# Self attention that begins seven steps earlier among the projections, with another order of passes in its weighted values

## The chip, the cores and the metric

The kernel runs on one core of one Trainium2 chip. The metric is the device time of one execution in microseconds (us). The core's engines are named as the profile names them: PE (TensorE, the matrix engine; PEld is its weight load), DVE (VectorE), ACT (ScalarE), POOL (GpSimd) and SP (SyncE, which here issues most DMAs).

## The reference

One decoder block on x (512 tokens of width 1024), all in float32. The part that the change touches first is a causal differential attention with four heads; each head has two score maps of 64 dimensions and 128 value dimensions:

```python
h = rms_norm(x, g_mix)
u, q, k, v, gate_logits = split(h @ w_in)
y_pool = causal_multiscale_pool(u, w_pool, pool_scale)
q, k = apply_rope(q), apply_rope(k)
p = softmax(where(mask, q·k / 8, -1e30))      # two maps per head
a = p[0] - lam * p[1]
o = rms_norm(a @ v, g_subln) * (1 - lam_init)
x = x + (concat(y_pool, o) * sigmoid(gate_logits)) @ w_out
```

A cross attention to a memory of 256 tokens follows (four heads of 256 dimensions), then a squared-ReLU MLP of width 4096, each behind an RMS norm and added to x, and a last RMS norm.

## The kernel before

**Data.** Activations lie transposed: 128 features on the partitions, the 512 tokens along the free axis. Every float32 operand is split into a high part, rounded to the matrix engine's fp32r type, and a low part, the rest; a product is three passes, high x high, high x low and low x high (`mm3`, L104). `split` (L110) makes the two parts, a copy on ACT (L111) and a subtraction on DVE (L112). The same is done for every block of weights (`prep`), after a DMA on SP's queue (`fetch`, L149), two tiles ahead of its use.

**Steps and tiles.** PE's order is written out by hand; the order of the other engines is planned by the framework from an estimate of when each instruction could run, earlier lines first, and `tc.high_priority()` ranks the instructions traced under it ahead of others. The planned orders are fixed when the kernel is built. A projection tile is eight steps of `mm3` (`tile_mm`, L290) into one of two PSUM banks `acc`. Each step advances a counter (`tick`), and work that `after(steps, ...)` has put on a list is issued on PE between two steps when its count is reached.

**The stage around the change.** `v_proj` (L375) makes the values in four PSUM banks (three `sc`, one `av`); three steps later `stats` (L394) computes the norm's factors, multiplies them into the cosine and sine tables and scales the values into `vr` (L264, L265). Then the tiles of `PLAN` (L41) run in order: k and q per head, the gates g, the pooling inputs u. `qk_proj` (L412) rotates a tile: four copies on ACT that swap quarters (L417), one product on DVE (L418), a product and a sum on POOL (L419, L420), two casts on ACT (L423, L425) and two subtractions on DVE (L424, L426). For k a swapped copy `z` is made by two DMAs on SP's queue (L430, L431). These halves share a ring of six buffers (`s`).

Behind the first two tiles, `START` steps on, the 16 blocks of scores (four heads, four blocks of 128 queries) are put on the list, `SPACE` = 6 steps apart. `scores` (L435) takes two PSUM banks of the three called `sc`; DVE adds the mask and finds the minimum (L445), ACT takes the exponential (L447), DVE inverts the sum (L449, L450), ACT scales one map (L451) and DVE combines the two (L452). `SOFTMAX` = 15 steps later `flip` (L456) transposes the block on PE (L463) and splits it into `at[0]` and `at[1]`; `ATTEND` = 3 steps after a head's last flip `attend` (L469) multiplies it with the values into the bank `av`, and `FINISH` = 6 steps later `finish` (L481) normalises and `merge` (L509) applies the gate. A gate tile costs ACT four passes (L500 to L504) and DVE two (L498, L503); a u tile works on DVE and POOL (L532 to L543).

**Cross attention.** For each head `cross_scores` (L673) makes scores and softmax, `cross_transpose` (L696) transposes and splits the result into a buffer `at`, and `cross_out` (L709) multiplies it with the memory's values into two `acc` banks, which are split into `xg`. The last of these calls are written out at L738 to L745.

Of the kernel before, what the change touches and what calls it, by code (L numbers as in the profile page):

```python
# [17 lines left out]
P = 128  # L18
# [3 lines left out]
NT = T // P  # L22
# [6 lines left out]
LAM_INIT = 0.8 - 0.6 * math.exp(-0.3 * 0)  # L29
WINDOWS = (2, 4, 8, 16)  # L30
PAD = 16
START, SPACE, SOFTMAX, ATTEND, FINISH, POOLING = 20, 6, 15, 3, 6, 23
MEMIN, EARLY, LATE = 16, [4, 5, 6, 0, 1], [2, 7, 3]
WARM = 8
ON_POOL = (1, 3, 5, 7), (1, 3, 5)
# [2 lines left out]
PARTS = "A11", "A12", "A21", "A22"  # L38
ORDER = "A11", "A12", "s1", "s2", "s3", "A22", "s4"
FIRST_ORDER = "A11", "s1", "A12", "s2", "s3", "A22", "s4"  # L40
PLAN = "k0 q0 q1 k1 q2 q3 g4 k2 g5 g6 k3 g7 u0 u1 u2 u3 g0 g1 g2 g3"  # L41

G_MIX, G_CROSS, G_MEM, G_MLP, G_FINAL, PSCALE, GSUB, LAMS = 0, 8, 16, 24, 32, 40, 44, 45
NG_COL = LAMS
# [6 lines left out]
def block_kernel(ctx: ExitStack, tc: tile.TileContext, x0g, xT, memT, wv, wm, wst, wckv, wpool, vecs, csts, outT):  # L51
    nc = tc.nc
# [23 lines left out]
    def sb(tag, shape, bufs, dt=F32):  # L76
        p = apool if tag in EARLY_TAGS else late["pool"] if tag in LATE_TAGS else pool
        return p.tile(shape, dt, tag=tag, name=nm(tag), bufs=bufs)

    def tmp(dt=F32):  # L80
        return sb("tmp", [P, T], 10, dt)

    def small(n=1):
        return sb("small", [P, 4], 24)[:, :n]

    def pair(tag, bufs):
        return sb(tag, [P, 2, T], bufs, F32R)

    def ps(tag, bufs):
        return psum.tile([P, T], F32, tag=tag, name=nm(tag), bufs=bufs)  # L90

    def acc():
        return ps("acc", 2)

    def f(ap):
        return ap.bitcast(F32)
# [7 lines left out]
    def mm3(o, lh, ll, rh, rl, start, stop):  # L104
        nc.tensor.matmul(o, lh, rh, start=start, stop=False)  # L105
        nc.tensor.matmul(o, lh, rl, start=False, stop=False)  # L106
        nc.tensor.matmul(o, ll, rh, start=False, stop=stop)  # L107
# [97 lines left out]
    def weights(i):  # L205
        far = 4 if i >= FIRST_UP else 0
        for j in range(i, i + 4 + far):
            if j < FIRST_UP or late:
                load(j)
        for j in range(i, i + 3 + far // 2):  # L210
            if j < FIRST_UP or late:
                prep(j)
        return ready.pop(i)


    def rsqrt(dst, ssum, scale, v, l, by=None):

        V.tensor_scalar(v, ssum, scale, EPS, op0=ALU.mult, op1=ALU.add)
        S.activation(l, ssum, AF.Ln, bias=eps, scale=scale)
        S.activation(dst, l, AF.Exp, scale=-0.5)  # L220
        S.activation(l, dst, AF.Square)
        V.scalar_tensor_tensor(l, l, -0.5, v, op0=ALU.mult, op1=ALU.mult)
        if by is not None:
            by(dst)
        V.scalar_tensor_tensor(dst, l, 1.5, dst, op0=ALU.add, op1=ALU.mult)

    def split_sq(sq, w, eng=V):
        hi = tmp(F32R)[:, :w]
        lo = tmp(F32R)[:, :w]
        split(hi, lo, sq, eng)  # L230
        return hi, lo

    def bcast_sum(o, hi, lo):
        nc.tensor.matmul(o, ones, hi, start=True, stop=False)
        nc.tensor.matmul(o, ones, lo, start=False, stop=True)
# [35 lines left out]
    def after(steps, fn, *args):  # L271
        heapq.heappush(due, (clock[0] + steps, uid[0], fn, args))
        uid[0] += 1
# [6 lines left out]
    def tick(n=1):  # L280
        for _ in range(n):
            clock[0] += 1
            run_due()
# [6 lines left out]
    def tile_mm(o, w, rhs, ks=range(KC), first=True, last=True):  # L290
        ks = list(ks)
        for n, k in enumerate(ks):
            c = slice(k * P, (k + 1) * P)
            mm3(o, w[0][:, c], w[1][:, c], rhs[k][0], rhs[k][1],
                first and n == 0, last and n == len(ks) - 1)
            tick()
# [5 lines left out]
    plan = [(e[0], int(e[1])) for e in  # L302
            PLAN.split()]
    where = {}
# [23 lines left out]
    def W(*key):  # L328
        return weights(where[key])
# [5 lines left out]
    st = {}  # L335
# [76 lines left out]
    def qk_proj(which, h):  # L412
        o = acc()
        tile_mm(o, W(which, h), xg)
        a, b = tmp(), tmp()
        for j in range(4):
            S.copy(b[32 * (j ^ 1):32 * (j ^ 1) + 32, :], o[32 * j:32 * j + 32, :])  # L417
        V.tensor_tensor(a, o, cos_r, op=ALU.mult)  # L418
        ROPE_E.tensor_tensor(b, b, sin_r, op=ALU.mult)  # L419
        nc.gpsimd.tensor_tensor(a, a, b, op=ALU.add)  # L420
        s = pair("s", 6)
        top, bot = slice(0, 64), slice(64, 128)
        S.copy(s[top, 0, :], a[top, :])  # L423
        V.tensor_tensor(s[bot, 0, :], a[top, :], f(s[top, 0, :]), op=ALU.subtract)  # L424
        S.copy(s[bot, 1, :], a[bot, :])  # L425
        V.tensor_tensor(s[top, 1, :], a[bot, :], f(s[bot, 1, :]), op=ALU.subtract)  # L426
        st[which, h] = s
        if which == "k":
            z = pair("s", 6)
            nc.sync.dma_start(f(z[top, :, :]), f(s[bot, :, :]))  # L430
            nc.sync.dma_start(f(z[bot, :, :]), f(s[top, :, :]))  # L431
            st["z", h] = z
# [36 lines left out]
    def attend(h):  # L469
        at = st["at", h]  # L470
        o = ps("av", 1)
        e = slice(h * P, (h + 1) * P)
        for b in range(NT):
            vh, vl = st["v"][b]
            mm3(o[:, b * P:], vh[:, e], vl[:, e], at[0][:, b, b * P:], at[1][:, b, b * P:],
                b == 0, b == NT - 1)
        sq = tmp()
        S.activation(sq, o, AF.Square)
        sp = split_sq(sq, T)

        def finish():  # L481
            s = ps("tr", 2)
            bcast_sum(s, *sp)
            y = tmp()
            rsqrt(y, s, 1.0 / P, sq, tmp(),
                  lambda r: V.scalar_tensor_tensor(r, o, st["gsub"], r, op0=ALU.mult, op1=ALU.mult))
            merge(4 + h, y)

        after(FINISH, finish)
# [19 lines left out]
    def merge(m, y):  # L509
        eng = MERGE_E if m < 4 else V  # L510
        eng.tensor_tensor(y, y, gate.pop(m), op=ALU.mult)
        pr = pair("mix", 8)
        split(pr[:, 0, :], pr[:, 1, :], y, MLO_E if m < 4 else V)
        mixed[m] = (pr[:, 0, :], pr[:, 1, :])
# [158 lines left out]
    def cross_scores(h):  # L673
        es = []
        for j in range(NT // 2):
            o = ps("sc", 3)
            for b in range(2):
                i = 2 * j + b
                tb = slice(i * P, (i + 1) * P)
                for c in range(2):  # L680
                    q, k = st["cq", 2 * h + c], st["mk", 2 * h + c]
                    mm3(o[:, b * M:(b + 1) * M], q[0][:, tb], q[1][:, tb], k[0], k[1], c == 0, c == 1)
            mx, sm = small(2), small(2)
            V.tensor_reduce(mx, o.rearrange("p (b m) -> p b m", b=2), axis=AX.X, op=ALU.max, negate=True)
            e = tmp()
            for b in range(2):
                c = slice(b * M, (b + 1) * M)
                S.activation(e[:, c], o[:, c], AF.Exp, bias=mx[:, b:b + 1], accum_out=sm[:, b:b + 1])
            V.reciprocal(sm, sm)
            for b in range(2):  # L690
                c = slice(b * M, (b + 1) * M)
                V.tensor_scalar(e[:, c], e[:, c], sm[:, b:b + 1], None, op0=ALU.mult)
            es.append(e)
        st["p", h] = es

    def cross_transpose(h):  # L696
        t = sb("at", [P, NT, T], 2, F32R)
        pt = (t[:, :MT, :], t[:, MT:, :])
        for j, e in enumerate(st["p", h]):
            tr = ps("tr", 2)  # L700
            for c in range(MT):
                for b in range(2):
                    nc.tensor.transpose(tr[:, (2 * c + b) * P:(2 * c + b + 1) * P],
                                        e[:, b * M + c * P:b * M + (c + 1) * P], ident)
            src = tr.rearrange("p (c t) -> p c t", c=MT)
            split(pt[0][:, :, j * M:(j + 1) * M], pt[1][:, :, j * M:(j + 1) * M], src)
        st["pt", h] = pt

    def cross_out(h):  # L709
        pt = st["pt", h]  # L710
        for dc in range(2):
            o = acc()
            m = 2 * h + dc
            c = slice((m % 4) * P, (m % 4) * P + P)
            for i in range(MT):
                vh, vl = st["mv", m // 4, i]
                mm3(o, vh[:, c], vl[:, c], pt[0][:, i, :], pt[1][:, i, :], i == 0, i == MT - 1)
            pr = pair("xg", 8)
            split(pr[:, 0, :], pr[:, 1, :], o)
            cross_o[m] = (pr[:, 0, :], pr[:, 1, :])  # L720
# [5 lines left out]
    for m in range(KC):  # L726
        o = acc() if m else ps("sc", 3)
# [9 lines left out]
            after(2, cross_transpose, m // 2 - 1)  # L737
    flush()  # L738
    cross_out(0)
    cross_scores(3)  # L740
    cross_transpose(2)
    cross_out(1)
    cross_out(2)
    after(2, cross_transpose, 3)
# [181 lines left out]
    for g in range(NG):  # L926
# [3 lines left out]
        for m in range(KC):  # L930
# [13 lines left out]
            if m < 2:  # L944
                o = acc()
# [8 lines left out]
            o = acc()  # L954
# [75 lines left out]
```

## Time and profile before

| | us |
|---|---|
| median of three runs | 722.4 (722.18 to 723.12) |
| the profiled execution | 722.57 |
| its span, first to last instruction | 720.8 |

The mean granted clock of PE is 0.998 of full speed. In a row of the timeline the first number is the start from the beginning of the span, the second the duration, both in us; a bracket at the end gives the idle time before the instruction and who ended it. A product's duration is modelled and longer than the distance to the next one, since PE overlaps them: with 512 columns it shows 0.39 us, and the next begins 0.23 us after it. In the view of waits a row reads: engine, tile and line that waited, for whom, us in total, times, the longest. In a view by stage a row gives busy time and instructions (x) of PE, PEld, DVE, ACT and POOL, then clock, share of the DMA engines and GB/s.

### The profile page before, as it was taken

Reading aid. Unit: us, or ns where it says so; the run is one execution under the profiler, and the core shown is the slowest. Engines: PE = TensorE matmul, PEld = TensorE weight load, DVE = VectorE, ACT = ScalarE, POOL = GpSimd, SP = SyncE. Lnnn points to the kernel's source line nnn. Section 1 sums busy time; section 2 is a strip of 40 time slices with the busy share of each in tenths; the row PEclk is TensorE's granted clock in tenths of the full one; section 3 lists DMA queues with packets and bytes.
Section 4 is the critical chain, followed back from the end, with each engine's and each line's share of the span. In section 5 each row is a group of like instructions: output and inputs, shape, how many; then the busy total and the mean of one; then the engine's idle time right before and its main releaser. Section 6 shows DMA issues by size and latency. Waiting matters only on the chain.

```text
span 720.8 us, 10378 instructions
## 1 busy us (share of the span) xinstructions
PE 706.5 (98%) x4016; PEld 617.0 (86%) x4016; DVE 510.6 (71%) x797; ACT 392.5 (54%) x646; POOL 66.9 (9%) x59
## 2 busy tenths in 40 slices
PE   8999999999999999999999999999999999999995
PEld 6887888788889888888879988999889988899894
DVE  7698999975888546572999954598446973589525
ACT  7498998676766434452865641355214641256432
POOL 0044112534000000000000000000000000000000
PEclk9999999999999999999999999999999999999999
DMA  8443223143525552113924850558216661305103
GB/s 315 151 118 116 88 75 116 60 146 119 176 88 176 181 170 83 65 58 143 246 79 127 237 164 30 150 111 294 89 33 167 205 182 58 88 30 161 45 1 116
DMA packets 28257, 91.09 MB, mean 126 GB/s; under 512 B 3089, under 2 KB 5137, under 8 KB 28209
## 3 DMA queue, kind: packets, MB, share of 16 engines
q1 hardware_dynamic: 25856, 81.92, 33.5%
q0 software_dynamic: 2352, 8.52, 7.0%
q8 instruction: 31, 0.51, 0.3%
q14 instruction: 18, 0.14, 0.1%
HBM read 86.24 MB, written 2.10 MB: 123 GB/s over the span
## 4 chain that ended last, share of the span: by engine, by line
PE 89%; DVE 5%; ACT 4%; issue 1%; DMA 0%; POOL 0%; DVEq 0%; SPq 0%; ACTq 0%
PE acc L105 17%; PE acc L106 17%; PE acc L107 17%; PE sc L105 11%; PE sc L106 11%; PE sc L107 11%; ACT tmp L447 1%; PE sc L386 1%; PE sc L388 1%; PE sc L390 1%; DVE tmp L445 1%; DVE wlo L112 1%; ACT tmp L417 1%; ACT whi L111 1%; DMA wraw<-wv 0%
## 5 line engine op out<-in xcount | busy, mean ns | idle before, releaser
L111 ACT CAST whi<-wraw 128x1024 fp32r<-128x1024 f32 (+1 forms) x94 | 97.2, 1035 | 107.5 <-PE acc L106 41.0
L105 PE MATMUL acc<-xg,whi 128*128 128x512 f32 x392 | 155.0, 395 | 0.0
L107 PE MATMUL acc<-xg,wlo 128*128 128x512 f32 x392 | 153.0, 390 | 0.0
L106 PE MATMUL acc<-xg,whi 128*128 128x512 f32 x392 | 152.7, 390 | 0.0
L112 DVE TENSOR_TENSOR wlo<-wraw,whi 128x1024 fp32r<-128x1024 f32 (+1 forms) x94 | 115.1, 1226 | 26.8 <-ACT whi L111 26.4
L107 PEld LDWEIGHTS acc<-xg,wlo 128*128 128x128 f32 x392 | 73.6, 188 | 15.8
L105 PEld LDWEIGHTS acc<-xg,whi 128*128 128x128 f32 x392 | 73.7, 188 | 14.5
L106 PEld LDWEIGHTS acc<-xg,whi 128*128 128x128 f32 x392 | 73.7, 188 | 14.3
L572 DVE TENSOR_TENSOR vr<-acc,vr 128x512 f32<-128x512 f32 x39 | 26.9, 690 | 76.5 <-PE acc L107 76.4
L105 PE MATMUL sc<-mix,whi 128*128 128x256 f32 (+1 forms) x184 | 54.2, 295 | 0.0
L107 PE MATMUL sc<-mix,wlo 128*128 128x256 f32 (+1 forms) x184 | 54.1, 294 | 0.0
L106 PE MATMUL sc<-mix,whi 128*128 128x256 f32 (+1 forms) x184 | 54.0, 294 | 0.0
L164 POOL DMA_DIRECT2D mraw<-wst x16 | 13.8, 864 | 429.1 <-DMA mraw<-wst 302.3
L111 ACT CAST whi<-mraw 128x1024 fp32r<-128x1024 f32 x24 | 25.0, 1052 | 45.9 <-PE acc L106 33.0
L890 DVE TENSOR_TENSOR tmp<-sc,tmp 128x512 f32<-128x512 f32 x56 | 37.5, 684 | 6.5 <-PE sc L107 6.4
L111 ACT CAST mhl<-wraw 128x1024 fp32r<-128x1024 f32 x19 | 20.0, 1052 | 34.4 <-PE acc L106 18.0
L106 PE MATMUL acc<-xg,mhl 128*128 128x512 f32 x96 | 37.4, 390 | 0.0
L105 PE MATMUL acc<-xg,mhl 128*128 128x512 f32 x96 | 37.4, 389 | 0.0
L107 PE MATMUL acc<-xg,mhl 128*128 128x512 f32 x96 | 37.4, 389 | 0.0
L107 PEld LDWEIGHTS sc<-mix,wlo 128*128 128x128 f32 x184 | 34.5, 188 | 1.1
L105 PEld LDWEIGHTS sc<-mix,whi 128*128 128x128 f32 x184 | 34.6, 188 | 1.0
L106 PEld LDWEIGHTS sc<-mix,whi 128*128 128x128 f32 x184 | 34.5, 187 | 1.1
(274 smaller groups left out, 1731.4 us busy)
## 6 DMA issues: line engine op xcount, KB each, us to landing
wraw<-wm SPq DMA_DIRECT2D x76, 512.0 KB, 3.5
mraw<-wst SPq DMA_DIRECT2D x24, 512.0 KB, 3.9
wraw<-wckv SPq DMA_DIRECT2D x16, 512.0 KB, 3.4
mraw<-wst POOLq DMA_DIRECT2D x16, 512.0 KB, 6.1
wraw<-wst SPq DMA_DIRECT2D x16, 512.0 KB, 3.4
s<-s SPq DMA_DIRECT2D x8, 256.0 KB, 3.7
vr<-xT SPq DMA_DIRECT2D x8, 256.0 KB, 4.5
outT<-mix SPq DMA_DIRECT2D x8, 256.0 KB, 2.4
```

What stands on the lines that cost most here:

```text
L105: nc.tensor.matmul(o, lh, rh, start=start, stop=False)
L106: nc.tensor.matmul(o, lh, rl, start=False, stop=False)
L107: nc.tensor.matmul(o, ll, rh, start=False, stop=stop)
L111: S.copy(hi, src)
L112: eng.tensor_tensor(lo, src, f(hi), op=ALU.subtract)
L164: nc.gpsimd.dma_start(r, part(n, then), accum_op=ALU.add)
L386: nc.tensor.matmul(o[i], xg[k][0][:, tb], wh[:, c], start=k == 0, stop=False)
L388: nc.tensor.matmul(o[i], xg[k][1][:, tb], wh[:, c], start=False, stop=False)
L390: nc.tensor.matmul(o[i], xg[k][0][:, tb], wl[:, c], start=False, stop=k == KC - 1)
L417: S.copy(b[32 * (j ^ 1):32 * (j ^ 1) + 32, :], o[32 * j:32 * j + 32, :])
L572: V.tensor_tensor(t, o, t, op=ALU.add)
L890: V.tensor_tensor(u[new], o, u[old], op=ALU.add)
```

## The change

Five edits. The first scores come 13 steps behind the first two tiles instead of 20, and everything listed after them moves with them. In the plan, k2 and k3 each change places with the gate tile ahead of them: `k2 g4 g5 k3 g6 g7` for `g4 k2 g5 g6 k3 g7`. The rotation becomes a function of its own, which runs at high priority for head 0's k and q. In `attend` the passes are ordered by factor over all four blocks of keys, so that the high part of the attention is used up before its low part is read. In the cross attention the transposes of head 2 come ahead of the scores of head 3.

```diff
-START, SPACE, SOFTMAX, ATTEND, FINISH, POOLING = 20, 6, 15, 3, 6, 23
+START, SPACE, SOFTMAX, ATTEND, FINISH, POOLING = 13, 6, 15, 3, 6, 23
...
-PLAN = "k0 q0 q1 k1 q2 q3 g4 k2 g5 g6 k3 g7 u0 u1 u2 u3 g0 g1 g2 g3"
+PLAN = "k0 q0 q1 k1 q2 q3 k2 g4 g5 k3 g6 g7 u0 u1 u2 u3 g0 g1 g2 g3"
...
     def qk_proj(which, h):
         o = acc()
         tile_mm(o, W(which, h), xg)
+        with tc.high_priority() if h == 0 else nullcontext():
+            rotate(which, h, o)
+
+    def rotate(which, h, o):
         a, b = tmp(), tmp()
         for j in range(4):
             S.copy(b[32 * (j ^ 1):32 * (j ^ 1) + 32, :], o[32 * j:32 * j + 32, :])
...
         at = st["at", h]
         o = ps("av", 1)
         e = slice(h * P, (h + 1) * P)
-        for b in range(NT):
-            vh, vl = st["v"][b]
-            mm3(o[:, b * P:], vh[:, e], vl[:, e], at[0][:, b, b * P:], at[1][:, b, b * P:],
-                b == 0, b == NT - 1)
+        for v, a in ((0, 0), (1, 0), (0, 1)):
+            for b in range(NT):
+                nc.tensor.matmul(o[:, b * P:], st["v"][b][v][:, e], at[a][:, b, b * P:],
+                                 start=v + a + b == 0, stop=a == 1 and b == NT - 1)
...
     flush()
     cross_out(0)
+    cross_transpose(2)
     cross_scores(3)
-    cross_transpose(2)
     cross_out(1)
     cross_out(2)
```

## The prediction

> **What bounds the kernel now.** I read the page's busy times first, then who TensorE (PE) waits for, then PE's instructions around each of those waits, then the other engines' instructions around the first scores.
>
> ```profile
> span 720.8 us, 10378 instructions
> ...
> PE 706.5 (98%) x4016; PEld 617.0 (86%) x4016; DVE 510.6 (71%) x797; ACT 392.5 (54%) x646; POOL 66.9 (9%) x59
> ```
>
> ```profile
> PE sc L442 <- DVE small L445: 0.9, 2, 0.7
> ...
> PE av L106 <- DVE at L112: 0.7, 2, 0.4
> PE acc L105 <- DVE xg L112: 0.4, 1, 0.4
> ...
> PE tr L463 <- DVE tmp L452: 0.3, 1, 0.3
> ```
>
> PE is the bound: busy in 98% of the span. The change neither adds nor drops a product, so only PE's waits can be won. The second view has few of them. Those that the change can touch are quoted: scores waiting for a PSUM bank (L442), weighted values waiting for the low half of the transposed attention (L106 of av), the cross attention waiting for a bank (acc L105), and one transpose waiting for its softmax (L463). It counts idle time from a modelled end, so I take each cost from start to start instead:
>
> ```profile
> 69.95 0.39 PE L107 MATMUL acc<-xg,wlo 128*128 128x512 f32 x1
> 70.66 0.41 PE L463 MATMUL tr<-cst,tmp 128*128 128x128 f32 x2 [0.32 <-DVE tmp L452]
> ...
> 83.69 0.48 PE L105 MATMUL av<-at,vr 128*128 128x512 f32 x1
> 84.58 0.50 PE L106 MATMUL av<-at,vr 128*128 128x512 f32 x1 [0.41 <-DVE at L112]
> 84.92 0.40 PE L107 MATMUL av<-at,vr 128*128 128x512 f32 x1
> ...
> 107.02 0.40 PE L105 MATMUL av<-at,vr 128*128 128x512 f32 x1
> 107.73 0.50 PE L106 MATMUL av<-at,vr 128*128 128x512 f32 x1 [0.32 <-DVE at L112]
> ...
> 124.52 0.28 PE L443 MATMUL sc<-s,s 128*128 128x256 f32 x1
> 124.99 0.38 PE L442 MATMUL sc<-s,s 128*128 128x256 f32 x1 [0.20 <-DVE small L445]
> ...
> 130.11 0.34 PE L443 MATMUL sc<-s,s 128*128 128x384 f32 x1
> 131.19 0.44 PE L442 MATMUL sc<-s,s 128*128 128x384 f32 x1 [0.75 <-DVE small L445]
> ...
> 322.11 0.40 PE L107 MATMUL acc<-at,mix 128*128 128x512 f32 x1
> 322.92 0.50 PE L105 MATMUL acc<-at,mix 128*128 128x512 f32 x1 [0.41 <-DVE xg L112]
> ```
>
> The steps of the work give the scale:
>
> ```profile
> 39.43 0.39 PE L105 MATMUL acc<-xg,whi 128*128 128x512 f32 x1
> ...
> 50.31 0.39 PE L105 MATMUL acc<-xg,whi 128*128 128x512 f32 x1
> ...
> 53.03 0.22 PE L442 MATMUL sc<-s,s 128*128 128x128 f32 x1
> ```
>
> Two tiles of eight steps lie between 39.43 and 50.31, so a step is 0.68 us and each of its three products 0.23. A start-to-start gap above 0.23 (512 columns), or above about 0.17 and 0.12 (384 and 256 columns, by the share of columns and a little more), is waiting. So the flip lost 70.66 - 69.95 - 0.23 = 0.48; the first weighted values 0.66 and, as the product behind a restart also starts late (84.92 - 84.58 = 0.34), 0.11 more; the second head's 0.48 and again 0.1; the scores 0.35 and 0.91; the cross attention 0.58. With 0.1 for each of the six restarts these are 0.6, 0.8, 0.6, 0.45, 1.0 and 0.7: 4.1 us in all. That is the most that the change can win.
>
> **The change, part by part.** The sum starts from the profiled execution, 722.57 us (span 720.8 and 1.8 around it). That is 0.17 above the median of the runs, 722.4, so a forecast made from it needs no correction worth making.
>
> *Order of passes in weighted values.* The low half `at[1]` is now first read by the ninth product of a head, not the second. The eight products ahead of it take at least 0.12 each, 0.9 us, more than the 0.66 and 0.48 that PE waited; both waits go. The twelve products are the same in number and width. **-1.4.**
>
> *Cross attention: transposes of head 2 ahead of the scores of head 3.* The late bank was released by a VectorE (DVE) subtraction which stood behind the one for those transposes:
>
> ```profile
> 321.58 0.68 DVE L112 TENSOR_TENSOR at<-tr,at 128x512 fp32r<-128x512 f32 x1
> 322.18 0.68 DVE L112 TENSOR_TENSOR xg<-acc,xg 128x512 fp32r<-128x512 f32 x1
> ```
>
> With the transposes issued one block earlier, the two `at` subtractions (0.68 each) can run while PE still does the scores, and the `xg` one no longer stands behind them. The 0.58 wait needs one of the two gone. What moves back is head 3's softmax, by one set of eight transposes; its own transposes come only after head 1 and 2's outputs, 24 products or 5.5 us. **-0.7**, bounds -0.7 and 0.
>
> *START 20 to 13: the late waits.* All scores, flips and weighted values move 7 x 0.68 = 4.8 us forward against the tiles. The score waits at 124.99 and 131.19 fall in the u tiles, where L445 stands in DVE's queue behind the evacuation of u0 and u1 and beside GpSimd (POOL). One u tile (8 steps) less has been evacuated when the same scores come. I take 1.2 of the 1.45 as won; bounds 1.45 and 0. The flip wait (0.6) belongs to head 0, whose chain moves into the rotations; **-1.2** and, half of it, **-0.3**.
>
> *START 13: the first scores.* Their step comes at 53.03 - 7 x 0.68 = 48.27. They need the rotated halves of q0 and, through two DMAs, the swapped copy of k0:
>
> ```profile
> 39.47 1.05 ACT L111 CAST whi<-wraw 128x1024 fp32r<-128x1024 f32 x1
> 40.40 0.71 ACT L264 ACTIVATE vr<-av,rrow 128x512 fp32r<-128x512 f32 x1
> 41.13 2.35 ACT L417 COPY tmp<-acc 32x512 f32<-32x512 f32 x4
> 43.51 0.62 ACT L423 CAST s<-tmp 64x512 fp32r<-64x512 f32 x1
> ...
> 45.92 2.35 ACT L417 COPY tmp<-acc 32x512 f32<-32x512 f32 x4
> 48.30 0.62 ACT L423 CAST s<-tmp 64x512 fp32r<-64x512 f32 x1
> ```
>
> ```profile
> 38.85 1.30 POOL L420 TENSOR_TENSOR tmp<-tmp,tmp 128x512 f32<-128x512 f32 x1
> ...
> 44.93 1.63 POOL L420 TENSOR_TENSOR tmp<-tmp,tmp 128x512 f32<-128x512 f32 x1
> ```
>
> ```profile
> 41.47 1.21 DVE L112 TENSOR_TENSOR wlo<-wraw,whi 128x1024 fp32r<-128x1024 f32 x1
> ...
> 45.43 1.68 DVE L426 TENSOR_TENSOR s<-tmp,s 64x512 fp32r<-64x512 f32 x1
> ...
> 50.22 1.68 DVE L426 TENSOR_TENSOR s<-tmp,s 64x512 fp32r<-64x512 f32 x1
> ```
>
> ```profile
> L424 DVE TENSOR_TENSOR s<-tmp,s x8: 685/688/1166, 44.2 to 110.5; 64x512 fp32r<-64x512 f32 x8
> L426 DVE TENSOR_TENSOR s<-tmp,s x8: 687/688/1677, 45.4 to 111.2; 64x512 fp32r<-64x512 f32 x8
> ...
> DMA to landing us min/median/max: 2.9/3.7/4.5
> ```
>
> Before, q0's halves end at 50.22 + 1.68 = 51.90, 3.6 us after the new step. Three things can bring them forward. (1) q0's copies start at 41.13, though its last product is issued just before 39.43: a weight cast and a scaling of v come first, 1.5 us, and the high priority ranks the rotation ahead of both. (2) q0's cast (48.30) stands behind q1's four copies, though POOL had its operand ready at 44.93 + 1.63 = 46.56: up to 1.7 us. It was already ahead of q1 in the program, so priority alone does not undo this; the planned order does, if the chain gets short enough in the plan. (3) The two subtractions took about 1.17 and 1.68 at the worst where the median is 0.69: 1.5 us, lost beside POOL's work on the next tile, which an earlier q0 avoids. All three make 4.7, so the wait may be nil; none leaves 3.6. For k0: its second DMA can go only after 45.43 + 1.68 = 47.11, so it lands near 50.8, 2.5 after the new step; but its cast at 43.51 had stood ready since 38.85 + 1.30 = 40.15, behind q0's copies, the same kind of order. The two waits overlap. I count (1) in full and a third of (2) and (3): 3.6 - 1.5 - 1.1 = **+1.0**, bounds 0 and 3.6.
>
> The Trainium skill, "SBUF — State Buffer", section "Who interferes with whom", says that a VectorE instruction with two SBUF inputs and a GpSimd one that reads SBUF lock each other out for the whole instruction. The trace agrees: L426 from 45.43 waits out POOL's sum to 46.56 and 0.69 more would be 47.25, against 47.11 measured. By that rule alone a q0 that still meets q1's two POOL operations could lose up to 1.6 on each subtraction, and the term would be nearer 2.8 than 1.0.
>
> *What priority pushes back.* The weight cast and its subtraction (39.47, 41.47) reuse the slot that q0 frees at 39.43 and serve the tile that starts at 50.31: ready at 42.68, 7.6 us of cover; a rotation put ahead of them costs 2.35 of copies and two casts of 0.62, so nothing is late. The scaled v frees the score banks when it is done at about 41.1, 7 us ahead of the new step; with 3.6 less cover it still is. Price 0; if that cover were gone, PE would wait for the difference.
>
> *k2 and k3 one place ahead.* Head 2's and 3's scores keep 21 steps after their k (20 before). Two gate tiles swap with two rotations, so ScalarE (ACT) has a rotation (2.35 + 1.24) among head 0's softmax where it had a gate's four passes, and seven rotations run without a gate between them. The two DMAs of each swapped k move with it on SP's queue past one weight load each; the swapped k2 still waits until head 1's scores free its buffer, in the same steps ahead of head 2's scores as before. In head 0's chain the flip wait above (0.48) is the nearest row for being late; it can come on three flips. I take **+0.4**, bounds 0 and 1.5.
>
> Sum: 722.57 - 1.4 - 0.7 - 1.2 - 0.3 + 1.0 + 0.4 = **720.4**.
>
> **The rivals.**
>
> *All waits go.* The rotation lands by 48.27 and the late DVE queue is relieved: 722.57 - 4.1 = 718.5. For it: the three savings for q0 exceed what is needed. Against it: each depends on an order of ACT that was the other way for k0 and q0 alike. Chance 0.20.
>
> *Only the two local edits pay.* ACT and DVE are as full earlier as they were late:
>
> ```profile
> 60.00:145.00 85.00, 83.00 (x401) 68.09 (x400) 75.27 (x189) 73.86 (x159) 25.87 (x19) 1.00 0.29 91
> ```
>
> In this stretch DVE is busy 75.3 of 85 us and ACT 73.9, and both engines' work is unchanged; the waits then only move to other scores. 722.57 - 1.4 - 0.7 + 1.0 = 721.5. Chance 0.22.
>
> *The first scores wait as long as they can* (the one that ends slower). If the plan leaves q0's cast behind q1's copies and its subtractions beside POOL, priority changes next to nothing: PE waits 3.6 us at L442 of head 0, the attention then lies only 1.2 us further forward than before, and the waits of flip and late scores stay. 722.57 + 3.6 - 2.1 = 724.1. It decides against the kernel from a first wait of 2.1 us on, and by more than 0.2% from 3.4 us on. For it: both casts stood behind the next tile's copies before. Chance 0.13. The Trainium skill, "TensorE: Matmul & The Clock Gate", section "HAM oscillation — how this bites in real kernels", says that an idle time of PE over some 3.4 us halves its clock. No wait here comes near that (the longest is 0.9), so the trace cannot tell. As a mechanism of this kernel, steps of 1.36 instead of 0.68 for as long as the wait itself lasted (3.6 us) would lose 1.8 us, so 725.9. I give that 0.03 of the 0.13.
>
> **How the numbers follow.** The forecast keeps 0.45. About 0.2% (1.4 us) is what a measurement of this kernel can tell from no change: faster means below 721.0, slower above 723.8. The forecast's own spread, about 1 us each way from its two unsure terms, puts 0.38 of its 0.45 below 721.0; with 0.20 for the case in which all waits go that is 0.58 faster. The other 0.07 and the 0.22 make 0.29 same. Slower 0.13. The range runs from 718.5 (all waits gone) to 722.8 (the local edits and a first wait of 2.3), leaving out the last rival and little else.
>
> **What would show it.** In the profile of the changed kernel: av L106 and acc L105 gone from PE's waits (orders of passes and transposes right); a wait at the first L442, near 48.3, of about 1.0 us, with q0's L417 starting near 39.7 and its L426 ending before 50; the L442 waits near 120 to 127 under 0.3 together; flips of head 0 waiting under 0.7 in all. Wrong would be a first wait above 2.5 us, new waits of tiles for their weights, or waits for gates or acc banks among the rotations.

## The result and the profile after

| | before | changed |
|---|---|---|
| median of four runs, us | 722.4 (722.18 to 723.12) | 731.75 (731.21 to 732.62) |
| profiled execution / span, us | 722.57 / 720.8 | 731.71 / 729.6 |

The ratio is 1.0125, interval 1.0112 to 1.0137: slower by 9.3 us, where the prediction said 2 us faster, and outside its range. Line numbers of the changed kernel are 4 higher behind the rotation (scores L446, their minimum L449, flip L467, the two subtractions of the rotation L428 and L430), and weighted values are now L479. First the head of the page, then PE's waits:

```profile
span 729.6 us, 10381 instructions
...
PE 710.4 (97%) x4016; PEld 618.3 (85%) x4016; DVE 511.4 (70%) x797; ACT 391.6 (54%) x646; POOL 68.7 (9%) x59
```

```profile
PE sc L446 <- DVE small L449: 2.0, 1, 2.0
PE sc L446 <- DVE s L428: 1.8, 1, 1.8
PE tr L467 <- DVE tmp L456: 1.5, 2, 1.2
PE sc L446 <- DVE s L430: 1.2, 1, 1.2
...
PE acc L105 <- DVE xg L112: 0.5, 1, 0.5
```

The engines do the same work as before. The wait of weighted values is gone from the list; the other three kinds of wait that the change was to remove are still there, none of them smaller, and two new ones stand at the first scores. Measured as in the prediction (distance between two starts less that of undisturbed products, summed over all 4016), the missing time was 7.5 us before and is 16.2 after: 8.7 of the 8.8 us of span. By place it is:

| term of the sum | predicted, us | measured, us |
|---|---|---|
| weighted values, order of passes | -1.4 | -1.1 |
| cross attention, swap | -0.7 | +0.1 |
| late score waits (both of head 3) | -1.2 | +0.9 |
| head 0's flips (about 0.4 of it at its last scores) | -0.3 | +1.6 |
| first scores | +1.0 | +3.5 |
| k2 and k3 a place ahead | +0.4 | see experiments |
| 135 to 165 us (u and gate tiles) | 0 | +2.1 |
| PE at half clock | 0 | +1.7 |

The measured terms make 8.8, against 8.7 in all.

**The first scores**, PE's timeline, then ACT's and DVE's:

```profile
48.04 0.39 PE L107 MATMUL acc<-xg,wlo 128*128 128x512 f32 x1
50.21 0.33 PE L446 MATMUL sc<-s,s 128*128 128x128 f32 x1 [1.78 <-DVE s L428]
50.37 0.28 PE L447 MATMUL sc<-s,s 128*128 128x128 f32 x1
51.88 0.33 PE L446 MATMUL sc<-s,s 128*128 128x128 f32 x1 [1.23 <-DVE s L430]
...
53.75 0.63 PE L105 MATMUL acc<-xg,whi 128*128 128x512 f32 x1
54.17 0.63 PE L106 MATMUL acc<-xg,whi 128*128 128x512 f32 x1
```

```profile
41.13 2.35 ACT L421 COPY tmp<-acc 32x512 f32<-32x512 f32 x4
...
45.92 2.35 ACT L421 COPY tmp<-acc 32x512 f32<-32x512 f32 x4
48.29 0.62 ACT L427 CAST s<-tmp 64x512 fp32r<-64x512 f32 x1
```

```profile
49.02 1.13 DVE L428 TENSOR_TENSOR s<-tmp,s 64x512 fp32r<-64x512 f32 x1
50.18 1.64 DVE L430 TENSOR_TENSOR s<-tmp,s 64x512 fp32r<-64x512 f32 x1
```

The scores were due at 48.04 + 0.23 = 48.27, as worked out. PE waits 1.94 for the first half of q0 and 1.40 more for the second, with the restart 3.5 us. ACT's copies and cast stand where they stood before, to 0.01 us (41.13, 45.92, 48.29 against 41.13, 45.92, 48.30): v's scaling (L264, from 40.40) is still ahead of q0's copies and q0's cast still behind q1's copies, at high priority too. DVE's second subtraction ends at 51.82 (before: 51.90). Nothing of the rotation came earlier; only PE did.

**Half clock.** Behind that, products that began 0.23 us after each other begin 0.42 apart (53.75 to 54.17). The view by stage for 53.60 to 56.90, of the changed kernel and then of the kernel before (PEclk is the first number behind POOL's):

```profile
53.60:56.90 3.30, 3.30 (x9) 2.53 (x9) 2.26 (x5) 2.71 (x6) 0.00 (x0) 0.51 0.00 0
```

```profile
53.60:56.90 3.30, 3.30 (x15) 2.69 (x15) 3.06 (x7) 2.75 (x8) 2.91 (x2) 1.00 0.46 159
```

PE is busy throughout, but gets 9 products done where it had done 15. The clock's record has the stretch as 3.41 us, from 53.4 to 56.8; half of that, 1.7 us, is lost.

**A late score**, PE and then DVE:

```profile
130.57 0.34 PE L447 MATMUL sc<-s,s 128*128 128x384 f32 x1
132.92 0.45 PE L446 MATMUL sc<-s,s 128*128 128x384 f32 x1 [2.00 <-DVE small L449]
```

```profile
130.70 0.68 DVE L536 TENSOR_TENSOR padu<-acc,rstd 128x512 f32<-128x512 f32 x1
131.32 1.20 DVE L112 TENSOR_TENSOR wlo<-wraw,whi 128x1024 fp32r<-128x1024 f32 x1
...
132.44 0.41 DVE L449 CUSTOM_DVE_ANT_0 tmp<-sc,cst 128x256 f32<-128x256 f32 x1
```

PE waits 2.2 us for a bank that DVE's minimum (132.44) must free. Ahead of that minimum DVE does a u tile's evacuation (0.68) and a weight subtraction (1.20). In the kernel before, at the wait of 0.91, DVE has both of them behind the minimum that frees the bank:

```profile
130.71 0.41 DVE L445 CUSTOM_DVE_ANT_0 tmp<-sc,cst 128x256 f32<-128x256 f32 x1
...
131.05 0.68 DVE L532 TENSOR_TENSOR padu<-acc,rstd 128x512 f32<-128x512 f32 x1
...
132.47 1.77 DVE L112 TENSOR_TENSOR wlo<-wraw,whi 128x1024 fp32r<-128x1024 f32 x1
```

**A late flip.** The flip at 77.07 comes 1.4 us late. DVE's combination for it runs at 76.31, as soon as ACT has scaled the second map (L455). DVE had the factor for that scaling ready at 70.34, but ACT does the next block's two exponentials and, of two rotations, four copies and two casts (3.6 us) first. DVE's factor, then ACT:

```profile
70.18 0.16 DVE L454 TENSOR_TENSOR small<-small,lam 128x1 f32<-128x1 f32 x1
```

```profile
73.17 1.76 ACT L421 COPY tmp<-acc 32x512 f32<-32x512 f32 x3
...
75.67 0.60 ACT L455 ACTIVATE tmp<-tmp,small 128x384 f32<-128x384 f32 x1
```

### The profile page after: what moved, and what is told of

The parts are those of the page before. It is cut to its first block, busy times and chain, and to the rows that moved or that the text cites. A ratio compares the mean times of both kernels' runs of the same rounds, so it can differ in the third digit from the quotient of the medians.

```text
span 729.6 us, 10381 instructions
## 1 busy us (share of the span) xinstructions
PE 710.4 (97%) x4016; PEld 618.3 (85%) x4016; DVE 511.4 (70%) x797; ACT 391.6 (54%) x646; POOL 68.7 (9%) x59
## 4 chain that ended last, share of the span: by engine, by line
PE 86%; DVE 7%; ACT 5%; issue 2%; DMA 0%; DVEq 0%; ACTq 0%
PE acc L105 16%; PE acc L106 16%; PE acc L107 16%; PE sc L105 11%; PE sc L106 11%; PE sc L107 11%; DVE wlo L112 1%; ACT tmp L421 1%; PE sc L386 1%; PE sc L388 1%; PE sc L390 1%; ACT whi L111 1%; PE av L479 1%; ACT tmp L451 1%; DVE s L430 1%
## 5 line engine op out<-in xcount | busy, mean ns | idle before, releaser
L112 DVE TENSOR_TENSOR wlo<-wraw,whi 128x1024 fp32r<-128x1024 f32 (+1 forms) x94 | 116.7, 1243 | 27.4 <-ACT whi L111 26.9
L107 PEld LDWEIGHTS acc<-xg,wlo 128*128 128x128 f32 x392 | 73.9, 189 | 16.0
```

The lines of the kernel that those rows point to most:

```text
L112: eng.tensor_tensor(lo, src, f(hi), op=ALU.subtract)
```

## The experiments

The first theory was that the early start costs what the first scores wait, with the half clock behind it, and that all else is small. The rival, which took its place, is that any shift of PE's order makes a new plan for DVE and ACT, which are nearly full here, and that PE then waits elsewhere. Each run stands beside runs of the kernel before on the same chip (medians 722.4 to 722.9).

**Start put back.** The changed kernel with

```diff
-START, SPACE, ... = 13, 6, ...
+START, SPACE, ... = 20, 6, ...
```

> The changed kernel with START back at 20, all else as changed. Theory A (the early start is the whole loss: 3.6 us of waiting at the first scores, 1.7 at half clock behind it, and the flip, score and tail waits that follow from it): all of these go, the new order of passes keeps its 1.1, so about 721.3. Rival B (k2 and k3 one place ahead make the later waits, some 4 us): only the first wait and the half clock go, about 725.5.

Measured 725.8 us, ratio 1.0054 (1.0035 to 1.0072). The first wait and the half clock are gone, so the early start costs 6 us here; but 3 us stay, near B's time. PE's waits show that other scores and flips took over, and that weighted values wait again (0.8 us) in spite of the new order of passes:

```profile
PE sc L446 <- DVE small L449: 1.6, 2, 1.0
PE tr L467 <- DVE tmp L456: 1.5, 2, 1.2
...
PE tr L467 <- DVE small L453: 1.1, 1, 1.1
...
PE av L479 <- DVE at L112: 0.8, 1, 0.8
```

**Plan put back.** The changed kernel with the old `PLAN`.

> The changed kernel with the old plan (g4 k2 g5 g6 k3 g7), START 13. A: no change that matters, 731.7 within 1. B: the flip, late score and tail waits go, about 727.5.

Measured 734.8 us, 1.0164 (1.0149 to 1.0179): both wrong. With START 13 the new plan is worth 3 us. The first wait is the same 1.94 and 1.40, but no half clock follows it; it follows a flip's wait of 2.5 us at 74.0 instead, and the scores wait for the DMAs of the swapped k (1.4 us).

**Plan alone.** The kernel before with the new `PLAN`.

> The kernel before with the new plan alone (START 20). B, as far as e1 against e4 supports it: the new plan costs 2.0 to 2.6 by itself, in flips and weighted values of heads 0 and 1, 724.8 (with the two av waits still there or longer). If the exchange of transposes and scores in the cross attention were the cause of the difference of e1 and e4: 722.4.

Measured 727.0 us, 1.0062 (1.0043 to 1.0081), more than the 724.8 expected. With START 20 the same exchange costs 4 us: 1.4 at the flip of head 0's last block, 1.95 at weighted values, and a half clock behind that. So the sign of the plan's price depends on the start. The four corners, all with the new order of passes (the upper left is the run that comes next, and lacks the priority and the swap, which further down turn out to be worth nothing):

| | old plan | new plan |
|---|---|---|
| START 20 | 723.2 | 725.8 |
| START 13 | 734.8 | 731.75 |

**Order of passes alone.** The kernel before with the edit in `attend`.

> The kernel before with the new order of passes in weighted values alone. A and B alike: the two waits of PE at av (0.66 and 0.48, with 0.1 of restart each) go, 721.1 to 721.4. If DVE's order is planned anew and the wait comes up elsewhere: 722.4.

Measured 723.2 us, 1.0012 (1.0001 to 1.0022): no gain, though the waits at weighted values are gone. Where it went shows in PE's waits:

```profile
PE sc L442 <- DVE small L445: 2.3, 2, 1.2
```

The same two score waits were 0.9 in all before. The first of them on PE, and what DVE does:

```profile
123.64 0.28 PE L443 MATMUL sc<-s,s 128*128 128x256 f32 x1
125.15 0.38 PE L442 MATMUL sc<-s,s 128*128 128x256 f32 x1 [1.23 <-DVE small L445]
```

```profile
124.21 0.68 DVE L532 TENSOR_TENSOR padu<-acc,rstd 128x512 f32<-128x512 f32 x1
124.81 0.28 DVE L445 CUSTOM_DVE_ANT_0 tmp<-sc,cst 128x128 f32<-128x128 f32 x1
```

PE reaches this place 0.88 us sooner than before (123.64, against 124.52), but DVE's minimum, which frees the bank, starts at 124.81 where it started at 124.65. DVE, ACT and POOL run their instructions in the same order in both traces, all 797, 646 and 59 of them, so this is no new plan: here DVE sets the pace, and what PE gains on the way it waits at the next meeting.

**Head 1's merge on POOL**, in the kernel of the last run, to take that load from DVE:

```diff
-        eng = MERGE_E if m < 4 else V
+        eng = MERGE_E if m < 4 or m == 5 else V
...
-        split(pr[:, 0, :], pr[:, 1, :], y, MLO_E if m < 4 else V)
+        split(pr[:, 0, :], pr[:, 1, :], y, MLO_E if m < 4 or m == 5 else V)
```

> e4 (before with the new order of passes) with the gating of head 1's result (a product of 0.69 and a subtraction of 1.3 on DVE) moved to POOL. If the score waits near 124 and 131 (2.6 us in e4) are DVE's queue in front of L445, they shrink by 1 to 2 us and the time is 721.5 to 722; if POOL's work beside DVE takes as much as it gives, 723.2.

Measured 727.1 us, 1.0067 (1.0046 to 1.0089): both wrong. The score waits grew to 4.7. On DVE the minimum now stands behind a u evacuation and a weight subtraction, as in the changed kernel:

```profile
131.40 0.67 DVE L532 TENSOR_TENSOR padu<-acc,rstd 128x512 f32<-128x512 f32 x1
...
132.09 1.20 DVE L112 TENSOR_TENSOR wlo<-wraw,whi 128x1024 fp32r<-128x1024 f32 x1
...
133.24 0.40 DVE L445 CUSTOM_DVE_ANT_0 tmp<-sc,cst 128x256 f32<-128x256 f32 x1
```

In the kernel before, both came behind the minimum (130.71, 131.05, 132.47). Moving one piece off DVE re-planned the rest for the worse.

**Filler.** The changed kernel with 14 more products, into a bank that nobody reads, ahead of the first scores.

```diff
+        if h == 0 and i == 0:
+            d = ps("tr", 2)
+            for j in range(14):
+                nc.tensor.matmul(d, xg[0][0][:, :P], xg[0][0], start=j == 0, stop=j == 13)
```

> The changed kernel with 14 products of 512 columns (0.23 us each, 3.2 us) put on PE right ahead of the first scores, into a bank that nobody reads. They fill the wait of 3.6 us and do no other work. If the half clock from 53.6 to 56.9 comes from the idle time of PE, the clock stays whole and the time falls by 1.7 to about 730.0, with the first wait on the records almost gone; if idle time is not what lowers it, the time stays at 731.7 and the rows at 0.43 us per product stay.

Measured 730.5 us, 1.0106 (1.0091 to 1.0122); near the expected time, but not as expected: 0.3 of the first wait is left and PE keeps its clock there, yet in the profiled execution the half clock comes at 132.0 instead, behind the score wait of 2.2.

**The order that priority was to give**, by explicit edges: q0's copies behind k0's casts, q1's copies behind q0's casts.

```diff
+        last = {("q", 0): ("k", 0), ("q", 1): ("q", 0)}.get((which, h))
+        with tc.issue_after(st["cast", last]) if last else nullcontext():
+            for j in range(4):
+                S.copy(b[32 * (j ^ 1):32 * (j ^ 1) + 32, :], o[32 * j:32 * j + 32, :])
...
+        st["cast", (which, h)] = S.copy(s[bot, 1, :], a[bot, :]).ins
```

> The changed kernel with two edges of issue order on ACT: q0's four copies behind k0's casts, q1's four copies behind q0's casts. Theory A (the planned order of ACT, not the speed of any engine, makes the first wait): q0's halves end near 48.5, the first wait falls from 3.3 to at most 0.5, no half clock follows it, so 731.7 - 4.5 = about 727; the flip and late waits stay. Rival C (the chain through POOL and the two DMAs is too long for 13 steps whatever the order): the first wait stays above 2 and the time above 729.5.

Measured 730.7 us (728.84 to 732.03), 1.0106 (1.0088 to 1.0124). The waits of the first scores fall from 3.3 to about 1.0 (0.60 and 0.44, besides 0.69 for a bank at 44.3), between what A and C said; A's 727 did not come. q0's cast on ACT and the two subtractions on DVE show what was won:

```profile
47.96 0.62 ACT L429 CAST s<-tmp 64x512 fp32r<-64x512 f32 x1 [2.45 <-POOL tmp L426]
```

```profile
48.61 0.69 DVE L430 TENSOR_TENSOR s<-tmp,s 64x512 fp32r<-64x512 f32 x1 [1.84 <-ACT s L429]
49.33 0.69 DVE L432 TENSOR_TENSOR s<-tmp,s 64x512 fp32r<-64x512 f32 x1
```

The second subtraction ends at 50.02, 1.8 us sooner than in the changed kernel (51.82). Only 0.3 of that is (2) of the prediction: the cast no longer stands behind q1's copies, but it starts at 47.96 against 48.29, since q0's copies start later (41.90) and POOL's sum for q0 now takes 2.25 us instead of 1.63 and ends at 47.92. Most of it, 1.4, is (3): with q1 held back POOL is idle beside the two subtractions, and they take 0.69 each instead of 1.13 and 1.64. In the profiled execution two other half-clock stretches (at 130.7 and 383.3) follow waits, and it took 731.3; an execution at a mean clock of 0.997, too high for any such stretch, took 728.84.

**START 16** in the changed kernel.

> The changed kernel with START 16. Theory A: the first scores come 3 steps (2.0 us) later, the first wait is 3.3 - 2.0 = 1.3, too short to lower the clock, so 731.7 - 2.0 - 1.7 = 728.0, with the other waits as they are. If the loss grows evenly with START (B: each step earlier costs the same), 725.8 + 4/7 x 5.95 = 729.2 with part of the half clock still there.

Measured 734.6 us, 1.0165 (1.0148 to 1.0182): both wrong. The first wait is 1.4, as worked out, but weighted values wait 5.2 us and a normalisation's sum (L235) 2.0. After this run the first wait could no longer be the whole story.

**No priority.** The changed kernel without `tc.high_priority()`.

> The changed kernel with only the high priority of the first rotation taken out. Theory A (priority ranked nothing anew, since the planned order of ACT, DVE and POOL up to the first scores is that of the kernel before): 731.7, the same two waits at the first scores (1.9 and 1.4) and the same half-clock stretch behind them. Rival B (priority did shorten the first wait, or moved work elsewhere): the first wait grows beyond 3.6 us or the time differs by more than 1 us, 729 to 734.

Measured 732.3 us, 1.0123 (1.0099 to 1.0146), the changed kernel's 1.0125. The waits are 1.94 and 1.40 again, and DVE, ACT and POOL run all their instructions in the same order with the priority and without it. The edit did nothing.

**The cross attention alone.** The kernel before with the exchanged lines.

> The kernel before with only the exchange of head 2's transposes and head 3's scores. Theory A (the late acc bank was not late because of that queue): the cross attention's wait stays near 0.6 and the time is 722.4. Rival B, the prediction's step: the 0.58 wait goes and the time is 721.7.

Measured 1.0002 (0.999 to 1.0014), and the wait is 0.65 where it was 0.58: no gain. DVE's timeline shows why:

```profile
321.49 0.62 DVE L692 TENSOR_SCALAR tmp<-tmp,small 128x256 f32<-128x256 f32 x2
322.02 0.68 DVE L112 TENSOR_TENSOR xg<-acc,xg 128x512 fp32r<-128x512 f32 x1
```

The subtraction for `xg` stood behind one for `at` (321.58, 0.68); now it stands behind the softmax of head 3 (0.62), which the exchange moved back.

**START 18 and START 22** in the kernel before, nothing else.

> The kernel before with START 18 instead of 20, nothing else. Theory A (any shift re-plans DVE and ACT, which are nearly full, so the first scores need not be late for the time to rise): due at 53.03 - 1.36 = 51.67, the first scores wait only about 0.5, yet waits of 1 us and more come up between 60 and 165 us, 723.5 to 728. Rival B (only the first scores' wait costs): 722.4 to 723.0.

> The kernel before with START 22 instead of 20. Theory A (START 20 is merely a place where the planned orders fit): the time rises here too, 723.5 to 728, although every need of the first scores is met earlier. Rival B (later scores only relieve): the waits of head 0's flip and the scores shrink, 721.0 to 722.4, a version that beats both kernels.

Measured 731.2 us, 1.0108 (1.0083 to 1.0132), and 732.3 us, 1.0125 (1.0104 to 1.0146). Theory A had the direction in both, but each time lies above its range of 723.5 to 728. This decides most. With START 18 the first scores begin at 51.6 and 51.9 with no wait but 0.1; with 22 they have 1.4 us more than before. Yet they lose 8.2 and 9.4 us, about as much as the whole change. PE's waits, of START 18 and then of START 22:

```profile
PE av L106 <- DVE at L112: 2.5, 3, 1.1
PE tr L463 <- ACT s L554: 1.7, 1, 1.7
PE av L105 <- ACT at L111: 1.3, 1, 1.3
...
PE sc L442 <- DVE small L445: 1.1, 1, 1.1
```

```profile
PE tr L463 <- DVE tmp L452: 1.9, 2, 1.4
PE tr L235 <- DVE tmp L112: 1.7, 1, 1.7
PE sc L442 <- DVE small L445: 1.7, 2, 1.4
PE acc L105 <- DVE tmp L418: 1.5, 1, 1.5
PE tr L234 <- ACT tmp L111: 1.5, 1, 1.5
```

Four and five kinds of places where before there was none above 0.9 in this stage. The missing time from 58 to 170 us is 4.6 before, 8.1 in the changed kernel, 11.0 with START 18 and 13.7 with 22, where a stretch at half clock is part of it; with START 18 one comes at 384, behind waits of 0.53 and 1.58.

**Less load.** The changed kernel, the kernel before and START 22, each without DVE's low part of the weights of the 20 tiles of the plan (their high part is read in its place).

```diff
+        elif 4 <= i < 24:
+            lo = hi = sb("whi", [P, D], 3, F32R)
...
+        elif 4 <= i < 24:
+            S.copy(hi, r)
```

> The changed kernel without DVE's subtraction for the low part of the weights of the 20 tiles of the plan: their high part is read in place of the low one, so the projections come out nearly doubled, and PE does the same products. DVE's work in the stage falls by about 20. Load theory: the waits behind 55 us (5.4 in all) shrink to under 2 and no half clock follows them; the first scores' wait shrinks a little, since one weight subtraction stood ahead of it; 722 to 726. Order theory: waits of 1 us and more stay between 60 and 165 us, 729 to 733.

> The kernel before with the same subtractions left out. Load theory: its waits between 60 and 135 us (0.48, 0.66, 0.49, 0.36, 0.91) shrink, 719.5 to 721.5. Order theory: new orders, new waits, 723 to 732.

> The kernel before with START 22 and the same subtractions left out. Load theory: the 9 us that START 22 cost nearly all go, 720 to 723. Order theory: 727 to 734.

Measured 725.8 us, ratio 1.0041 (1.0026 to 1.0056); 721.8 us, 0.9987 (0.9977 to 0.9996); and 725.6 us, 1.0039 (1.0026 to 1.0052): the first in the range of the load theory, the two others between the ranges. The view by stage for 60 to 145 us, of the changed kernel and then of its lighter version (PE, PEld, DVE, ACT, POOL):

```profile
60.00:145.00 85.00, 81.20 (x393) 66.57 (x392) 72.11 (x177) 72.81 (x156) 20.67 (x16) 1.00 0.27 84
```

```profile
60.00:145.00 85.00, 83.79 (x407) 68.91 (x406) 62.74 (x169) 75.15 (x160) 20.21 (x17) 1.00 0.30 95
```

With 9.4 us less DVE work in this stretch PE does 14 more products. The waits behind 55 us fall from 6.0 to 1.8 us in the changed kernel, and from 10.7 to 4.8 with START 22; the kernel before, which had little to win, gains 0.9. Against that lighter kernel before, the changed kernel is 4.0 us slower where it was 9.3, and START 22 3.8 where it was 9.4. So over half of either loss goes when DVE has 20 subtractions less. These runs don't part load from order, though: the lighter kernels have new orders too (ACT does the same 646 instructions in each pair, but from 34 us on in another order). What stays shows in waits: the first scores still wait 2.9 us in the lighter changed kernel, with their half clock, and START 22 still waits 1.4 at 108 us and 1.6 and 1.0 at 140, with another half clock. The three times did not come together, so less load on DVE alone does not make the three plans alike.

## Why the prediction was wrong

**What bounds the kernel** was right: PE, and only its waits matter. But "4.1 in all. That is the most that the change can win" was read as the scale of what can happen. The risk was of another size: DVE and ACT at 75.3 and 73.9 of 85 us left little slack, and the missing time from 58 to 170 us grew from 4.6 to 13.7 us (1.7 of it at half clock) by two steps of delay alone, START 22. The sum put nothing at the stretch from 135 to 165 us (+2.1) and at the half clock (+1.7).

**Order of passes, -1.4.** Near in size (-1.1): one weighted product still waits, 0.24 us at 86.8. But "both waits go" holds only while the low half comes within those eight products, about 1.2 us; with other plans the ninth product waits, 0.95 us in the run with START put back and 5.2 us over three heads with START 16. And it was wrong as a term of a sum: alone it gained nothing (+0.8), since what PE gains there the next scores wait.

**Cross attention, -0.7.** The step that failed is "The 0.58 wait needs one of the two gone". One was gone, and the softmax that "moves back" took its place on DVE, which the text had said and not priced.

**Late waits, -1.2.** The step that failed is "One u tile (8 steps) less has been evacuated when the same scores come". The wait at 125 us went, but the one at 130 us grew from 0.9 to 2.2, because DVE now does a u evacuation and a weight subtraction ahead of the minimum. The prediction had read that wait as standing behind the evacuation of u1; in the kernel before that evacuation came behind the minimum (131.05 against 130.71). Moving all scores forward by 4.8 us does not move them out of DVE's queue; DVE's order is planned anew, and it is about as full earlier (75.3 of 85 us).

**Flips, -0.3.** The prediction saw that head 0's "chain moves into the rotations" and counted it as half a gain. It was a loss: the scaling for the flip at 77.07 stood on ACT behind four copies and two casts of rotations and ran 5.3 us after its factor was ready, and that flip waits 1.4 us.

**First scores, +1.0.** The due time, 48.27, and the upper bound, 3.6, were right (3.5 measured). The step that failed is "the high priority ranks the rotation ahead of both": the kernel without it waits the same 3.3 us, and ACT's order is that of before. "I count (1) in full and a third of (2) and (3)" should have been nothing. As for (3), the two subtractions met POOL's work on q1 and took 1.13 and 1.64. The explicit edges, which cut these waits to 1.0, won most by (3), 1.4, and only 0.3 by (2). (1) stays untried: in that run q0's copies start later than before (41.90 against 41.13). By the rule of the Trainium skill, "SBUF — State Buffer", section "Who interferes with whom", the prediction had worked out 2.8 for a q0 that meets that work, and this came nearer than the sum.

**Two gate tiles, +0.4.** Neither size nor sign: +2.6 with START 20 (725.8 against 723.2), -3.0 with START 13.

**The rivals.** "The first scores wait as long as they can" was what happened at 48 us, and its rider, the half clock, came too. It had 0.13, and 725.9 was 6 us short, for it counted the rest of the stage as staying as it was ("the waits of flip and late scores stay"). No rival said that the waits elsewhere would grow; START 18, with no first wait and 8.2 us lost, shows that this alone is enough.

**What stays open.** Why START 20 with the old plan fits so well is not settled: 18 and 22 with that plan lie 8.2 and 9.4 us above it, 13 lies 12.4 above it with that plan and 9.3 with the new one, and 16 was tried with the new one alone (11.7). How much of this is DVE's load and how much its order is open too; no run changed one and kept the other. That the planner's estimates differ from the real durations is likely, since it put work ahead of the critical minimum that could have waited; no run tested its estimates. None of the versions beat the kernel before, but for the one that leaves part of its own work out (721.8).

## What to carry to other kernels

When the engines that serve the bound one are as busy in a stage as here (75.3 and 73.9 of 85 us) and their order is planned, treat an edit to when work is issued as a new plan: do not sum local savings, and try the neighbouring values of the constant (here 18 and 22) before believing that one direction is better. A priority only helps where the planned order really changes: look at the order, or set it by explicit edges. Ask of each wait that is removed which instruction of the loaded engine will be next in line.

## What the runs showed of the hardware

**The clock follows a fixed grid of 3.413 us.** In the clock's record of every profiled execution the stretches are whole multiples of it, but for the last, which the end cuts off: in the changed kernel 47.79 us at full clock (14 windows), 3.41 at half, 669.01 at full (196). What matters is how much of one such window PE lacks, not the length of one wait. In 17 kernels' profiled executions 14 windows, one of them at half clock itself, were followed by one at half clock while work went on: 13 had about 1.9 to 2.7 us of missing time, one (the changed kernel's, 50.0 to 53.4) had 1.61. Over 40 other windows at full clock had 1.0 us or more missing; the most were 1.93 and 1.94, the rest had about 1.9 or less. So the point lies near 1.9 us, some 56% of a window, as an estimate from these counts; it is not sharp. A wait of 2.2 us that straddles two windows (the changed kernel's at 130.6: 1.11 and 1.06) was followed by no half clock. The grid starts at another moment in each execution, so the same waits are followed by a half clock in one and not in another: without priority the same 1.94 and 1.40 brought two windows of it (51.2 to 58.0), in the changed kernel one. The Trainium skill, "TensorE: Matmul & The Clock Gate", section "HAM oscillation — how this bites in real kernels", speaks of waits that cross a window of about 3.4 us; these runs agree with the window's length and show that about 1.9 us inside it were mostly enough.
